# Two of four weight-block sums of a seven-product feed-forward stage, made by adding transfers from SBUF to SBUF instead of by VectorE

## The chip, the cores and the metric

The kernel runs on one core of a Trainium2 chip. The metric is the device time of one execution in microseconds; the kernel before has a median of 2433.65 us over three runs (2429.97 to 2434.26). Instructions and waits are read from one profiled execution, which took 2429.76 us.

## What is computed

One decoder layer over 512 positions of width 2048, in float32: a combined input projection, dilated attention and a pooling mixer, gates, an output projection, a normalisation, and a feed-forward part of hidden width 8192. The change is in the first matrix product of the last line but one:

```python
def reference(x, positions, w_in, w_pool, ..., w_ff1, w_ff2, ln_ff_g, ln_ff_b):
    ...
        x = layer_norm(DEEPNORM_ALPHA * x + mix, ln_mix_g[layer], ln_mix_b[layer])
        f = jnp.square(jax.nn.relu(x @ w_ff1[layer])) @ w_ff2[layer]
        x = layer_norm(DEEPNORM_ALPHA * x + f, ln_ff_g[layer], ln_ff_b[layer])
    return x
```

## The kernel before

Every matrix product works with float32 operands that are split into a high part, rounded to the matmul's format, and a low remainder: ScalarE writes the high part (line 87), VectorE subtracts it (line 88), and TensorE makes three products (high by high, high by low, low by high). For weights the parts are called wh and wl; both have three buffers, so the split of a piece can run at most two pieces ahead of the piece that TensorE works on.

The first feed-forward product runs by a scheme of seven products in place of eight (after Strassen and Winograd): the 512 positions are two halves, the 2048 rows of the weight two halves, and the hidden columns come in 16 groups of 512, each of two halves. Group 0 is made in the ordinary way; groups 1 to 15 are the units (class FUnit). A unit has four weight blocks, "11", "12", "21" and "22" (row half, column half), 128x2048 elements each, in four buffers (w1). It makes the products in the order M1, M5, M6, M3, M7, M2, M4. Each product is two pieces (FPiece, half of the rows each), so a unit has 14 pieces, j = 0 to 13, of 24 matmuls each.

The weights that M5, M6, M7 and M4 need are sums, made in place: 11 += 12 beside the splits of M1's pieces, 11 += 22 beside those of M5 (then M6 uses 11), 12 += 22 for M7, and 11 += 21 for M4. Each sum is two halves, one VectorE instruction of 128x1024 each (line 618).

The order of everything beside the matmuls is written out by hand, piece by piece: `fill` gives the splits up to piece j + 2, then `beside(u, j, last)` gives what belongs to piece j, and then the matmuls of piece j follow. `u.give(n, half)` hands a buffer on: it issues, on SyncE's queue, the load of the next unit's block into the half that is no longer used (line 613, 0.5 MB a load). The buffer of 22 is given at j = 4 and 6, that of 12 at j = 6 and 7, that of 21 at j = 8 and 9 and that of 11 at j = 10 and 11.

The result of a unit, the hidden blocks, is kept in one tile hpR: `block` (line 672) writes into it at j = 10, 12 and 13. During the next unit its combinations (line 548) are made and stored to memory for the second feed-forward product (`h_parts_out`, from line 550): at j = 5 and again at j = 7 ScalarE writes the high parts into hpH, a tile with one buffer, VectorE subtracts, and POOL stores both, h_parts<-hpH and h_parts<-hpR, 896 KB each (line 555). POOL's queue also carries the loads and stores of the residual rows (`y_load`, `y_rows`: lines 518 to 536). An engine works through its own queue strictly in order, so an instruction that waits holds up all behind it. SyncE's loads go through DMA queue q1, POOL's transfers through q0; both use the same 16 DMA engines.

Of the kernel before, what the change touches and what calls it, by code (L numbers as in the profile page):

```python
# [13 lines left out]
OP = mybir.AluOpType  # L14
# [54 lines left out]
def decoder_layer(ctx: ExitStack, tc: tile.TileContext, x, xt, positions, w_in, w_pool, pool_scale,  # L69
                  w_branch_attn, w_branch_pool, w_out, ln_mix_g, ln_mix_b, w_ff1, w_ff2,  # L70
                  ln_ff_g, ln_ff_b, consts, vectors, out, h_parts, h_rest, y_norm, y_parts):
    nc = tc.nc
# [443 lines left out]
    def y_load(t, n):  # L516
        c = slice(n * 512, (n + 1) * 512)
        nc.gpsimd.dma_start(low["u"][:, 1], y_norm[t, :, c])
        nc.gpsimd.dma_start(low["g"][:, 0], bcast(ln_mix_g, c))
        nc.gpsimd.dma_start(low["g"][:, 1], bcast(ln_mix_b, c))  # L520

    def y_rows(t, n):
        c = slice(n * 512, (n + 1) * 512)
        v, g, b = low["u"][:, 1], low["g"][:, 0], low["g"][:, 1]
        stt = nc.vector.scalar_tensor_tensor
        stt(v, v, ALPHA, g, op0=OP.mult, op1=OP.mult)
        stt(v, b, ALPHA, v, op0=OP.mult, op1=OP.add)
        if t >= 2 and n % 2:
            nc.gpsimd.dma_start(g, y_parts[t - 2, :, c])
            return lambda: y_rest(t, c)  # L530
        nc.gpsimd.dma_start(y_parts[t, :, c], v)
# [133 lines left out]
    def beside(u, j, last):  # L665

        v = {m: p.rearrange("p (n t) -> p n t", n=2) for m, p in u.ps.items()}
        m1, m5, u2 = low["m"][:, 0], low["m"][:, 1], low["u"][:, 0]
        act = nc.scalar.activation

        def block(slot, in0, in1, op):
            nc.vector.tensor_tensor(R[u.g][:, :, slot], in0.rearrange("p (n t) -> p n t", n=2), in1, op=op)

        def relu(a, b):
            act(R[u.g][:, :, a:b], R[u.g][:, :, a:b], AF.Relu)

        if j == 0:
            last.done()
        elif j == 2:
            act(m1, u.ps["M1"], AF.Copy)  # L680
        elif j == 4:
            act(m5, u.ps["M5"], AF.Copy, scale=-1.0)
            u.sum("12", "22", 0)
            u.give(0, 0)
        elif j == 6:
            act(u2, u.ps["M1"], AF.Copy, scale=-1.0)
            u.sum("12", "22", 1)
            u.give(0, 1)
            u.give(1, 0)
        elif j == 7:  # L690
            u.give(1, 1)
            if chunks:
                y_load(*chunks[0])
        elif j == 8:
            u.sum("11", "21", 0)
            u.give(2, 0)
        elif j == 9:
            u.sum("11", "21", 1)
            u.give(2, 1)
        elif j == 10:  # L700
            block(0, m5, v["M1"], OP.subtract)
            u.give(3, 0)
        elif j == 11:
            u.give(3, 1)
            if chunks:
                u.rest = y_rows(*chunks.pop(0))
        elif j == 12:
            block(1, u2, v["M5"], OP.subtract)
        elif j == 13:
            block(3, m1, v["M2"], OP.add)  # L710
            relu(0, 2)
        if j == 3 and last.rest:
            last.rest()
        if j in last.out:
            last.out[j]()
# [98 lines left out]
    def bcast(v, c=slice(0, DM)):  # L814
        return bass.AP(tensor=v.tensor, offset=v.offset + c.start, ap=[[0, P], [1, c.stop - c.start]])
# [188 lines left out]
    for p in fpieces:  # L1004
        fill(pos[2])
        beside(p.u, p.j, last)
        if p.u is funits[0] and p.j == 0:
            y_p3()
            funits[0].get("21")
        if p.u in funits[1:3] and p.j in (0, 4):  # L1010
            (y_load(*chunks[0]) if p.j == 0 else y_rows(*chunks.pop(0)))
        p.mult()
        pos[2] += 1
        if p.u is funits[-1] and p.j in (3, 5, 7):
            for m in {3: (0, 1), 5: (2, 3), 7: (4, 5)}[p.j]:
                h_load(0, m)
        if p.j == 13:
            last = p.u
# [89 lines left out]
```

## Time and profile before

| | value |
|---|---|
| median of three runs | 2433.65 us |
| the profiled execution | 2429.76 us |
| its span, first to last instruction | 2428.0 us |
| granted TensorE clock, mean | 0.997 |
| TensorE busy | 2392.9 us (99%) |
| VectorE busy | 1585.5 us (65%) |
| ScalarE busy | 963.1 us (40%) |
| POOL busy | 168.7 us (7%) |

The seven-product stage lies between about 1170 and 1793 us of the span. A unit takes some 41 us there, so a stretch of that length shows one turn of the order. TensorE's busy share counts waiting matmuls poorly, since matmuls overlap; the length of a unit and TensorE's listed waits tell more.

### The profile page before, as it was taken

What the parts mean: (1) busy time and instruction counts of PE and PEld (TensorE: products, weight loads), DVE (VectorE), ACT (ScalarE), POOL (GpSimd) and SP (SyncE); (2) the same over time, 40 slices, a digit from 0 to 9 for tenths busy, and PEclk for the clock granted to TensorE, in tenths of its full rate; (3) what the DMA queues carried; (4) which work ended last, traced back from release to release, by engine and by line L of the source; (5) the groups of instructions that cost most, each with busy time, mean ns of one, the idle gap of its engine ahead of it and who ended that gap; (6) DMA issues with size and microseconds to landing.
All of it is one profiled execution on the core that took longest, in us unless ns stands there. A gap on an engine that the chain in (4) does not pass through costs nothing.

```text
span 2428.0 us, 31729 instructions
## 1 busy us (share of the span) xinstructions
PE 2392.9 (99%) x13096; PEld 2078.2 (86%) x13096; DVE 1585.5 (65%) x1641; ACT 963.1 (40%) x1030; POOL 168.7 (7%) x256
## 2 busy tenths in 40 slices
PE   9999999999999999999899999999999999999998
PEld 7888888877788888888899999999988888888886
DVE  4532345555533334346888888888877988889886
ACT  4323311244432223126555555555554333333330
POOL 0000000000000000000112121111121000110000
PEclk9999999999999999999999999999999999999999
DMA  6232333222223333347577667676797556675642
GB/s 210 87 96 100 104 96 98 93 79 78 78 87 96 96 100 116 123 156 234 170 218 228 223 212 236 204 240 196 251 342 251 183 181 225 211 240 178 207 163 94
DMA packets 202880, 399.33 MB, mean 164 GB/s; under 512 B 12272, under 2 KB 74864, under 8 KB 201968
## 3 DMA queue, kind: packets, MB, share of 16 engines
q1 hardware_dynamic: 164272, 257.84, 33.0%
q0 software_dynamic: 36160, 135.28, 16.4%
q10 hardware_dynamic: 2304, 4.20, 0.5%
q8 instruction: 102, 1.67, 0.3%
q14 instruction: 42, 0.34, 0.0%
HBM read 329.11 MB, written 68.16 MB: 164 GB/s over the span
## 4 chain that ended last, share of the span: by engine, by line
PE 75%; issue 11%; DMA 6%; DVE 5%; ACT 2%; POOL 1%; POOLq 0%; SPq 0%; DVEq 0%; ACTq 0%
PE mm L147 43%; PE pp L800 20%; PE mm L663 5%; PE pp L845 4%; DMA w<-in_w_ff 2%; DVE wl L88 2%; DMA h_parts<-hpH 2%; DMA h_parts<-hpR 1%; DVE hpR L88 1%; PE sc L351 1%; PE tp L383 1%; ACT wh L87 1%; DMA low<-in_ln_mix_g 1%; ACT hpH L87 1%; DMA wr<-in_w_out 0%
## 5 line engine op out<-in xcount | busy, mean ns | idle before, releaser
L88 DVE TENSOR_TENSOR wl<-wr,wh 128x1024 fp32r<-128x1024 f32 (+1 forms) x228 | 277.5, 1220 | 566.9 <-ACT wh L87 566.3
L87 ACT ACTIVATE wh<-w 128x1024 fp32r<-128x1024 f32 x406 | 427.3, 1058 | 521.1 <-PE pp L800 295.0
L88 DVE TENSOR_TENSOR wl<-w,wh 128x1024 fp32r<-128x1024 f32 x406 | 494.5, 1221 | 109.6 <-ACT wh L87 107.8
L800 PE MATMUL pp<-wh,hop 128*128 128x512 f32 x1568 | 483.3, 389 | 1.2 <-ACT hpR L624 1.2
L87 ACT ACTIVATE wh<-wr 128x1024 fp32r<-128x1024 f32 (+1 forms) x228 | 240.4, 1055 | 611.4 <-PE mm L147 565.3
L147 PE MATMUL mm<-aH,wh 128*128 128x512 f32 (+1 forms) x1024 | 396.3, 387 | 1.3 <-ACT wh L87 1.3
L147 PE MATMUL mm<-aH,wl 128*128 128x512 f32 (+1 forms) x1024 | 386.8, 378 | 5.1 <-DVE wl L88 5.1
L147 PE MATMUL mm<-aL,wh 128*128 128x512 f32 (+1 forms) x1024 | 386.1, 377 | 0.0
L800 PEld LDWEIGHTS pp<-wh,hop 128*128 128x128 f32 x1568 | 294.4, 188 | 62.4 <-ACT hpR L624 1.4
L800 PE MATMUL pp<-wl,hop 128*128 128x512 f32 x784 | 305.4, 390 | 1.3 <-DVE wl L88 1.3
L663 PE MATMUL mm<-aH,wl 128*128 128x256 f32 x960 | 273.0, 284 | 7.0 <-DVE wl L88 7.0
L663 PE MATMUL mm<-aH,wh 128*128 128x256 f32 x960 | 271.9, 283 | 0.0
L663 PE MATMUL mm<-aL,wh 128*128 128x256 f32 x960 | 271.9, 283 | 0.0
L147 PEld LDWEIGHTS mm<-aH,wl 128*128 128x128 f32 x1024 | 193.5, 189 | 41.7 <-DVE wl L88 6.3
L147 PEld LDWEIGHTS mm<-aH,wh 128*128 128x128 f32 x1024 | 193.7, 189 | 39.1 <-ACT wh L87 2.5
L147 PEld LDWEIGHTS mm<-aL,wh 128*128 128x128 f32 x1024 | 193.8, 189 | 36.9 <-issue 1.9
L663 PE MATMUL mm<-ysH,wl 128*128 128x256 f32 x720 | 205.3, 285 | 6.0 <-DVE wl L88 6.0
L663 PE MATMUL mm<-ysH,wh 128*128 128x256 f32 x720 | 204.1, 283 | 0.0
L663 PE MATMUL mm<-ysL,wh 128*128 128x256 f32 x720 | 203.9, 283 | 0.0
L663 PEld LDWEIGHTS mm<-aH,wl 128*128 128x128 f32 x960 | 184.3, 192 | 8.7 <-DVE wl L88 8.4
L663 PEld LDWEIGHTS mm<-aH,wh 128*128 128x128 f32 x960 | 184.5, 192 | 0.0
L663 PEld LDWEIGHTS mm<-aL,wh 128*128 128x128 f32 x960 | 184.4, 192 | 0.0
(175 smaller groups left out, 3360.3 us busy)
## 6 DMA issues: line engine op xcount, KB each, us to landing
w<-in_w_ff SPq DMA_DIRECT2D x232, 512.0 KB, 10.8
wr<-in_w_in SPq DMA_DIRECT2D x127, 512.0 KB, 3.6
hop<-h_parts POOLq DMA_DIRECT2D x98, 512.0 KB, 7.1
h_parts<-hpH POOLq DMA_DIRECT2D x28, 896.0 KB, 9.3
h_parts<-hpR POOLq DMA_DIRECT2D x28, 896.0 KB, 9.2
wr<-in_w_out SPq DMA_DIRECT2D x40, 512.0 KB, 3.6
wr<-in_w_ff SPq DMA_DIRECT2D x32, 512.0 KB, 4.0
wr<-in_w_branch_pool SPq DMA_DIRECT2D x16, 512.0 KB, 3.7
```

Source lines behind the costliest of these rows:

```text
L87: nc.scalar.activation(dst_h, src, AF.Copy)
L88: nc.vector.tensor_tensor(dst_l, src, dst_h.bitcast(F32), op=OP.subtract)
L147: nc.tensor.matmul(o, l, r, start=first and j == 0, stop=last and j == 2)
L351: nc.tensor.matmul(p[:, :n], qT[h][:, qb * P:(qb + 1) * P], kT[h][:, :n], start=True, stop=True)
L383: nc.tensor.matmul(p[:, k * P:], vt["v"][:, k, h * HD:(h + 1) * HD], pT[h][:, k, k * P:], start=k == 0, stop=k == 3)
L663: nc.tensor.matmul(o, l, r, start=first, stop=self.j % 2 == 1 and k == 3 and i == 2, skip_group_check=True)
L800: nc.tensor.matmul(u.ps[:, t], l, r, start=q + j == 0, stop=q == 3 and j == 2)
L845: nc.tensor.matmul(o, l, r, start=first and i == 0, stop=last and i == 2)
```

## The change

In `beside`, the four instructions of a unit that add the second pair of sums are taken out, and two transfers take their place. They are issued by POOL and add their source to their destination, whole blocks at once (128x2048): 12 += 22 at j = 0 and 11 += 21 at j = 3. What is given on, and when, stays as it was.

```diff
         if j == 0:
             last.done()
+            nc.gpsimd.dma_start(u.b["12"], u.b["22"], accum_op=OP.add)
         elif j == 2:
             act(m1, u.ps["M1"], AF.Copy)
         elif j == 4:
             act(m5, u.ps["M5"], AF.Copy, scale=-1.0)
-            u.sum("12", "22", 0)
             u.give(0, 0)
         elif j == 6:
             act(u2, u.ps["M1"], AF.Copy, scale=-1.0)
-            u.sum("12", "22", 1)
             u.give(0, 1)
             u.give(1, 0)
         elif j == 7:
             u.give(1, 1)
             if chunks:
                 y_load(*chunks[0])
+        elif j == 3:
+            nc.gpsimd.dma_start(u.b["11"], u.b["21"], accum_op=OP.add)
         elif j == 8:
-            u.sum("11", "21", 0)
             u.give(2, 0)
         elif j == 9:
-            u.sum("11", "21", 1)
             u.give(2, 1)
```

VectorE's queue in the second unit, from the split of M3's first half on (w_ and a number name the four weight buffers), before:

```order
L88 TENSOR_TENSOR wl<-w_7708,wh 128x1024
L618 TENSOR_TENSOR w_7705<-w_7705,w_7708 128x1024
L88 TENSOR_TENSOR wl<-w_7708,wh 128x1024
L88 TENSOR_TENSOR hpR<-hpR,hpH 128x1792
L88 TENSOR_TENSOR wl<-w_7705,wh 128x1024
L618 TENSOR_TENSOR w_7705<-w_7705,w_7708 128x1024
L88 TENSOR_TENSOR wl<-w_7705,wh 128x1024
L88 TENSOR_TENSOR hpR<-hpR,hpH 128x1792
L88 TENSOR_TENSOR wl<-w_7869,wh 128x1024
L618 TENSOR_TENSOR w_7669<-w_7669,w_7869 128x1024
L88 TENSOR_TENSOR wl<-w_7869,wh 128x1024
L618 TENSOR_TENSOR w_7669<-w_7669,w_7869 128x1024
```

And the same stretch after:

```order
L88 TENSOR_TENSOR wl<-w_7708,wh 128x1024 x2
L88 TENSOR_TENSOR hpR<-hpR,hpH 128x1792
L88 TENSOR_TENSOR wl<-w_7705,wh 128x1024 x2
L88 TENSOR_TENSOR hpR<-hpR,hpH 128x1792
L88 TENSOR_TENSOR wl<-w_7870,wh 128x1024 x2
L88 TENSOR_TENSOR wl<-w_7669,wh 128x1024
```

The four L618 sums are gone and the splits and hpR subtractions keep their order.

POOL's queue over one later unit, before (in brackets the semaphores that a transfer waits for: DMAHW those of SyncE's loads, DMASW those of POOL's own transfers):

```order
L555 DMA h_parts<-hpH 128x7x256 [waits DMASW4_49,Activation_49]
L555 DMA h_parts<-hpR 128x7x256 [waits DMASW5_49,DVE_49]
L518 DMA low<-y_norm 128x512 [waits DMASW6_49,DMASW3_49]
L519 DMA low<-in_ln_mix_g 128x512 [waits DMASW7_49]
L520 DMA low<-in_ln_mix_b 128x512 [waits DMASW0_49]
L555 DMA h_parts<-hpH 128x7x256 [waits DMASW1_49,Activation_49]
L555 DMA h_parts<-hpR 128x7x256 [waits DMASW2_49,DVE_49]
```

And after:

```order
L679 DMA w_7705<-w_7708 128x2048 [waits DMAHW5_49,DMAHW6_49,DMAHW4_49,DMAHW7_49,DMASW2_49,DVE_49]
L694 DMA w_7669<-w_7870 128x2048 [waits DMAHW0_49,DMAHW1_49,DMASW3_49,DVE_49]
L555 DMA h_parts<-hpH 128x7x256 [waits DMASW4_49,Activation_49]
L555 DMA h_parts<-hpR 128x7x256 [waits DMASW5_49,DVE_49]
L518 DMA low<-y_norm 128x512 [waits DMASW6_49,DMASW1_49]
L519 DMA low<-in_ln_mix_g 128x512 [waits DMASW7_49]
L520 DMA low<-in_ln_mix_b 128x512 [waits DMASW0_49]
L555 DMA h_parts<-hpH 128x7x256 [waits Activation_49]
```

Both adding transfers (L679 and L694) stand ahead of the unit's four stores on POOL and wait for weight loads and for VectorE.

## Rows read from the trace of the kernel before

**Rows 1.** Windows: length, busy of PE, PEld, DVE, ACT, POOL; PEclk, DMA share, GB/s.
```profile
1215.77:1752.17 536.40, 528.40 (x4371) 525.18 (x4370) 462.36 (x437) 300.65 (x299) 85.80 (x115) 1.00 0.69 223
...
1384.70:1425.15 40.45, 40.45 (x339) 40.38 (x338) 35.10 (x34) 23.06 (x23) 6.13 (x8) 1.00 0.65 214
1589.71:1630.04 40.33, 40.33 (x338) 40.33 (x337) 36.08 (x35) 23.60 (x24) 6.13 (x8) 1.00 0.67 223
```

**Rows 2.** Waits of PE, 1215.77 to 1752.17: total us, times, longest us.
```profile
PE mm L663 <- DVE wl L88: 7.9, 11, 1.6
```

**Rows 3.** Groups by line: the sums (busy us, mean ns | idle before, releaser).
```profile
L618 DVE TENSOR_TENSOR w<-w,w 128x1024 f32<-128x1024 f32 x120 | 146.7, 1222 | 19.8 <-DMA w<-in_w_ff 18.0
```

**Rows 4.** Waits of ACT (1215.77 to 1752.17), then of SP (1190 to 1780).
```profile
ACT wh L87 <- DVE w L618: 90.8, 45, 4.9
...
SPq L613 <- DVE w L618: 423.4, 60, 19.0
```

**Rows 5.** Chain of waits, 1355 to 1390: start us, us, what.
```profile
1359.93 8.36 DMA h_parts<-hpH
...
1368.38 1.71 ACT hpH L87
...
1370.11 2.04 DVE hpR L88
```

**Rows 6.** Waits of PE, units of 1341.98 to 1384.70 and of 1425.15 to 1466.5.
```profile
PE mm L663 <- DVE wl L88: 1.9, 2, 1.6
...
PE mm L663 <- DVE wl L88: 0.6, 1, 0.6
```

**Rows 7.** DMA issues at 1402, 1359, 1442 and 1565: KB each, us to landing.
```profile
h_parts<-hpH POOLq DMA_DIRECT2D x1, 896.0 KB, 5.9
...
h_parts<-hpH POOLq DMA_DIRECT2D x1, 896.0 KB, 8.4
...
h_parts<-hpH POOLq DMA_DIRECT2D x1, 896.0 KB, 7.4
...
h_parts<-hpH POOLq DMA_DIRECT2D x1, 896.0 KB, 7.5
```

**Rows 8.** GB/s of all DMA, 1387 to 1404 in 40 equal slices.
```profile
GB/s 272 217 159 137 108 87 67 29 0 0 0 0 0 0 0 0 0 0 0 0 0 0 0 39 0 0 0 0 0 0 0 0 0 0 0 0 0 55 152 188
```

**Rows 9.** Timelines of DVE, SP, ACT, POOL about 1400: start us, us, engine, line.
```profile
1397.19 1.22 DVE L88 TENSOR_TENSOR wl<-w,wh 128x1024 fp32r<-128x1024 f32 x1
...
1401.95 0.37 SPq L613 DMA_DIRECT2D w<-in_w_ff  x1
...
1402.23 1.06 ACT L87 ACTIVATE wh<-w 128x1024 fp32r<-128x1024 f32 x1 [0.28 <-PE mm L663]
...
1402.25 0.97 POOL L555 DMA_DIRECT2D h_parts<-hpH  x1 [20.51 <-ACT hpH L87]
```

**Rows 10.** DMA queues, 1350 to 1473: packets, MB, share of 16 engines.
```profile
q0 software_dynamic: 4000, 14.68, 34.3%
q1 hardware_dynamic: 12672, 12.58, 32.3%
```

**Rows 11.** The same, 1404 to 1408.
```profile
q0 software_dynamic: 299, 1.16, 72.8%
```

**Rows 12.** Waits of DVE, then of ACT, 1215.77 to 1752.17.
```profile
DVE hpR L672 <- DMA h_parts<-hpR: 6.4, 6, 1.5
...
ACT hpH L87 <- DMA h_parts<-hpH: 5.5, 8, 1.7
```

**Rows 13.** Timeline of DVE, 1384.6 to 1394, in brackets the idle time before.
```profile
1384.57 0.69 DVE L672 TENSOR_TENSOR hpR<-low,mm 128x512 f32<-128x512 f32 x1 [1.30 <-DMA h_parts<-hpR]
...
1392.33 1.23 DVE L88 TENSOR_TENSOR wl<-w,wh 128x1024 fp32r<-128x1024 f32 x1 [1.68 <-ACT wh L87]
```

**Rows 14.** DMA queues and issues, 1407.7 to 1411.7.
```profile
q0 software_dynamic: 258, 0.97, 99.2%
...
w<-in_w_ff SPq DMA_DIRECT2D x2, 512.0 KB, 16.0
```

## The prediction

> **What bounds the kernel now.** I first read the windows of the first feed-forward stage. Over thirteen units of the seven-product scheme (1215.77 to 1752.17 us) TensorE is busy 528.4 of 536.4 us at a granted clock of 1.00 (the 2.4 GHz level), VectorE 462.4 us, and the 16 DMA engines 69% [rows 1]. One unit that nothing disturbs takes 40.33 us [rows 1], so thirteen would take 524.3 us: the stage has only 536.4 - 524.3 = 12.1 us, 0.93 us per unit, that any relief of VectorE could give back. The waits say that TensorE stands for one thing only, the low part wl that VectorE writes: 7.9 us in 11 waits [rows 2] (the rest of the 12.1 us is in smaller gaps). VectorE is 86% busy here, yet its own load is not what is late. I followed the chain of waits back from one such wait: POOL issues the store of the high parts of hidden blocks (h_parts<-hpH) at 1359.93; it lands 8.36 us later; only then may ScalarE write the next hpH into the same buffer (1.71 us), then VectorE subtracts (2.04 us) [rows 5], and the wl of the next piece stands behind that subtraction. In this unit TensorE waited up to 1.6 us, in the unit where the same store took 7.4 us it waited 0.6 us, and in the unit where it took 5.9 us it did not wait at all [rows 1, 6, 7]. So there is a limit of about 6.8 us from issue to landing (8.4 - 1.6 and 7.4 - 0.6), and each us above it is a us of TensorE. Call this **place A**. **Place B** is at the unit's end: VectorE's write of a hidden block into hpR (L672) waits for the last h_parts<-hpR store, 6.4 us in 6 waits [rows 12]; in one such case the write started at 1384.57 and the wl that ends the chain of VectorE and ScalarE work behind it started at 1392.33 [rows 13], and TensorE just did not have to wait for it (the unit of 1384.70 to 1425.15 is full [rows 1]). Both places hang on when stores land, not on how much VectorE adds.
>
> **What the change removes.** Four of the eight L618 sums of a unit leave VectorE: 60 of 120 in the stage, 1.222 us each [rows 3], so 60 x 1.222 = 73 us of VectorE, or 4.9 us per unit. ScalarE's waits for L618 (90.8 us) fall by perhaps half, and SyncE, which today waits for L618 before it may reload a buffer (423.4 us, 60 times) [rows 4], waits for VectorE's wl and for the adding transfer instead. All this lies between the sixth and the tenth piece. Place A's chain (landing, hpH, subtraction, wl) holds none of the removed sums, nor does place B's. So the gain that I count on TensorE's path is 0; the 12.1 us are its ceiling.
>
> **What it adds.** Two adding transfers per unit from POOL, 128x2048 f32 (1.05 MB) each; the trace of before has none, so I bound one from both sides. A plain pass of q0 cost 2.5 us per MB while stores ran (1.16 MB in 72.8% of 4 us) [rows 11], and 2.9 us per MB over three units (14.68 MB in 34.3% of 123 us) [rows 10]. The lower end is one pass, 1.05 x 2.5 = 2.6 us of all 16 engines; the upper is three passes (source, destination, write back, none overlapped) at 2.9, 9.1 us. I take two, since an add must read two tiles and a plain store already reads and writes in its one pass: 5.2 us. The Trainium skill ("Collectives: The Full Stack", Part 3) says the same of the reduce that DMA engines make: two source reads, the add itself free, at about 31 GB/s per engine; by it the estimate is 2 x 1.05 / (16 x 0.031) = 4.2 us, and the total below would be about 14 us less. No run here shows such an add yet.
>
> *First adding transfer (12 += 22).* It is issued once the buffers of 22 have landed. There the DMA engines fall idle: from about 1390 to 1402 hardly a byte moves [rows 8]. With 5.2 us of bytes and 3.6 us of overhead (a store's 5.9 us [rows 7] less 0.92 MB x 2.5) it lands some 9 us after issue, near 1399, ahead of the reload of 22 (1401.95) and of the first wh that reads 12 (1402.23) [rows 9]. That idle stretch is its cover; about 3 us are left, and past it each us delays M7 by one. Cost 0. On POOL, y_load stands behind it in the two units that load at their start; its rows are wanted four pieces later. Cost 0.
>
> *Second adding transfer (11 += 21).* It waits for the wl of M6's second half, which ends at 1397.19 + 1.22 = 1398.41; the hpH store follows on POOL at 1402.25 [rows 9], so its bytes stand 3.8 us behind in the same queue. The adding transfer needs 5.2 us, and the 0.5 MB reload issued at 1401.95 shares the engines (1.3 us): the store is pushed by 5.2 - 3.8 = 1.4 to 2.7 us; I take 2.0. **Place A:** landing 5.9 + 2.0 = 7.9, so 7.9 - 6.8 = 1.1 us of wait in a unit that does not wait today. Three of the thirteen units land it in 7.4 to 8.4 us today [rows 7]; there it is about 2.9 us. Mean (10 x 1.1 + 3 x 2.9) / 13 = 1.5 us. **Place B:** from the second adding transfer on, the engines have 5.2 us more to move and start 1401.95 - 1398.41 = 3.5 us earlier, so the last store lands 1.7 us later. Reloads freed about 3 us earlier by the missing sums compete with the stores: 0 if the stores keep the engines, as in the 4 us in which q0 had 99.2% while two loads had been issued [rows 14], or 1.5 us at an even share. I take 0.7, between the two, since over three units q1's packets take nearly as much time as q0's [rows 10]. The Trainium skill ("DMA: Bandwidth & Descriptors", Queues, rings and completion order) says that an engine goes round robin between its queues, packet by packet; by it the 1.5 us would hold, and the 4 us of the row above show otherwise. So the store lands 2.4 us later, of which TensorE has already stood 1.5 us at place A: 0.9 more.
>
> **Sum.** Per unit 1.5 (A) + 0.9 (B) + about 0.5 (the half of today's 0.93 that I put down to B, unchanged) = 2.9 us against 0.93 now: +2.0 us; over 14 units that store, +28 us. POOL's two more issues (under 1 us each, as its stores' are) and the other stages cost 0. The profiled execution took 2429.76 us (span 2428.0): 2429.8 + 28 = 2458. It lies 3.9 us below the median 2433.65, so the forecast on the median is **2462 us**.
>
> **Rivals.**
> *(1) The adding is slow.* Three passes, or an adder slower than the stream: q0 and q1 take 42.2 + 39.7 us of three units now [rows 10], 27.3 us per unit; with 2 x 9.1 that is 45.5 us and the DMA engines become the bound, +5.2 us per unit, +72 us: 2506; at 12 us per transfer 51.3 us, +150 us. For it: nothing in the trace prices an add. Against it: a stream that reads two tiles has no need of a third pass. It decides from about 6.5 us per transfer, where 27.3 + 2 x 6.5 reaches 40.3.
> *(2) Faster.* The adding costs about one pass (2.6 us) and is over before the store's bytes come; the reloads, free 3 us earlier, move in the stretch that is idle now, so the stores of the second half land earlier and both places close: up to 12 us less, 2422 to 2428. It decides where an adding transfer moves its bytes within the 3.8 us ahead of the store. For it: the idle stretch is there and VectorE gets 4.9 us per unit. Against it: it must do its two reads at twice the rate of q0's stores.
> *(3) No change.* Adding near 3.5 us: A is pushed by under 1 us, the earlier reloads give it back: 2429 to 2438.
>
> **How the numbers follow.** The forecast (slower, 2439 to 2506, likeliest 2462) gets 0.53, rival 1 beyond that 0.15, rival 2 0.18, rival 3 0.14. A measurement of this kernel can tell about 0.2% (4.9 us) from no change; so faster 0.18, same 0.14, slower 0.68. The range goes to 2424, which leaves out the better half of rival 2, and to 2520, which leaves out an adder at 10 us and more.
>
> **What would show it.** Right: VectorE's L618 group shows 60 sums, 73 us less; the undisturbed unit stays near 40.3 us but few are left; h_parts<-hpH from the unit's first half lands at 7.5 to 9 us, ScalarE's wait for it grows from 5.5 us to 20 us or more and VectorE's wait for h_parts<-hpR from 6.4 us [rows 12], TensorE's waits for wl reach 30 us or more, and the DMA share goes from 69% to about 90%. Wrong: an adding transfer that lands within 6 us of its issue and TensorE's waits at or below 7.9 us (rival 2 or 3); or adding transfers of 12 us and more, a stage near 100% DMA share, and M7's wh waiting for the first of them (rival 1).

## The result: 56 us slower, twice the forecast loss

The changed kernel takes 2490.0 us (median of four, 2488.0 to 2492.0), the kernel before 2433.86 us beside it: ratio 1.0236, 95% interval 1.0224 to 1.0248. The forecast was slower by 28 us (2462, range 2424 to 2520). The direction and the place held; the size was short by half.

**Where the time went.** The profiled execution took 2488.0 us, its span is 2486.2 us. Two windows of each trace split the span: the seven-product stage (units 1 to 15), and all that follows it. First the kernel before, then after; the columns are those of [rows 1].

```profile
1169.71:1790.26 620.55, 607.51 (x5018) 603.26 (x5017) 532.15 (x500) 349.58 (x351) 101.81 (x140) 1.00 0.69 222
1790.26:2428.00 637.74, 624.12 (x2762) 516.28 (x2760) 536.93 (x430) 234.97 (x222) 59.53 (x104) 0.99 0.59 203
```

```profile
1170.81:1840.36 669.55, 626.83 (x5017) 620.90 (x5017) 468.29 (x440) 350.57 (x351) 128.87 (x169) 0.97 0.85 250
1840.36:2486.20 645.84, 625.18 (x2762) 517.42 (x2760) 537.00 (x430) 235.27 (x222) 60.27 (x105) 0.99 0.59 203
```

The stage is 49.0 us longer, what follows 8.1 us, and what goes before 1.1 us. In the stage TensorE's idle time went from 620.55 - 607.51 = 13.0 us to 669.55 - 626.83 = 42.7 us: **29.7 us of waiting**. Its busy time rose by **19.3 us** for the same 5017 or 5018 matmuls, and the mean granted clock fell from 1.00 to 0.97. So the loss has three main parts: waits 29.7, busy time 19.3 (most of it slower matmuls, as shown below), the stage that follows 8.1.

**VectorE got what was meant, and TensorE nothing.** The sums in the lines of groups, and both transfers in the list of DMA issues of 1223.65 to 1761.08 (KB each, median us to landing):

```profile
L618 DVE TENSOR_TENSOR w<-w,w 128x1024 f32<-128x1024 f32 x60 | 73.5, 1225 | 2.1
```

```profile
w<-w POOLq DMA_DIRECT2D x24, 1024.0 KB, 8.3
h_parts<-hpH POOLq DMA_DIRECT2D x24, 896.0 KB, 9.4
h_parts<-hpR POOLq DMA_DIRECT2D x24, 896.0 KB, 10.3
```

60 sums are left of 120 [rows 3]: 73 us off VectorE. Its windows above show 63.9 us less in the stage.

**What TensorE waits for.** The waits of 1223.65 to 1761.08 (12 units), against [rows 2], [rows 4] and [rows 12], which cover thirteen units:

```profile
ACT hpH L87 <- DMA h_parts<-hpH: 70.3, 12, 7.3
...
PE mm L663 <- DVE wl L88: 20.1, 13, 1.8
...
PE mm L663 <- ACT wh L87: 12.9, 9, 2.3
...
DVE hpR L672 <- DMA h_parts<-hpR: 3.6, 3, 2.6
...
ACT wh L87 <- DVE w L618: 2.4, 2, 1.2
```

ScalarE's wait for the store h_parts<-hpH, 5.5 us before, is 70.3 us: once in each of the 12 units. TensorE waits 20.1 + 12.9 = 33.0 us, 2.75 us per unit, for the wl and the wh behind that. Place B's wait went down, from 6.4 to 3.6 us.

**One unit, step by step.** The chain of waits of 1455 to 1490, then the timelines of ScalarE, VectorE and TensorE:

```profile
1464.95 9.92 DMA h_parts<-hpH
...
1474.95 1.71 ACT hpH L87
...
1478.64 2.35 DVE wl L88 x2
```

```profile
1474.95 1.70 ACT L87 ACTIVATE hpH<-hpR 128x1792 fp32r<-128x1792 f32 x1 [6.55 <-DMA h_parts<-hpH]
1476.56 2.93 ACT L87 ACTIVATE wh<-w 128x1024 fp32r<-128x1024 f32 x3
...
1476.69 2.02 DVE L88 TENSOR_TENSOR hpR<-hpR,hpH 128x1792 f32<-128x1792 f32 x1 [7.03 <-ACT hpH L87]
...
1477.65 0.39 PE L663 MATMUL mm<-aH,wh 128*128 128x256 f32 x1 [1.59 <-ACT wh L87]
...
1479.90 0.58 PE L663 MATMUL mm<-aH,wl 128*128 128x256 f32 x1 [1.75 <-DVE wl L88]
```

It is the chain of [rows 5]. The store of the unit's first half lands 9.92 us after its issue; ScalarE, in order, stands 6.55 us before the next hpH, and the splits of the coming piece stand behind it: TensorE waits first for wh, then for wl.

**The prediction's limit of 6.8 us holds.** Over the 12 units the store of the first half lands 7.96, 8.01, 8.09, 9.30, 9.40, 9.64, 9.87, 9.92, 10.04, 10.07, 10.65 and 11.08 us after issue. Each less 6.8 us, summed, is 32.4 us; the waits measured are 33.0 us. The 0.6 us between the two are one wait, at 1544.96, that follows the longest wait of place B (2.6 us, to 1535.92).

**Behind the waits the clock falls.** Windows of a short unit, a long one, and three short stretches:

```profile
1405.29:1447.10 41.81, 40.58 (x339) 40.38 (x337) 30.70 (x30) 23.24 (x23) 7.98 (x10) 1.00 0.84 247
1447.10:1493.53 46.43, 43.09 (x338) 42.68 (x337) 31.76 (x31) 23.24 (x23) 8.52 (x11) 0.93 0.87 262
1478.24:1485.07 6.83, 5.17 (x24) 5.17 (x25) 4.48 (x5) 1.54 (x3) 1.01 (x1) 0.50 0.98 344
1420.00:1423.41 3.41, 3.41 (x30) 3.41 (x30) 2.18 (x2) 3.13 (x3) 0.69 (x1) 1.00 1.03 175
...
1570.40:1573.81 3.41, 3.41 (x18) 3.41 (x17) 2.12 (x3) 0.00 (x0) 0.00 (x0) 0.50 1.03 403
```

From the second of the two waits of the unit above on, the granted clock is 0.50, the level of 1.2 GHz, for 6.83 us. The last two rows are two stretches of equal length: 30 matmuls at full clock, 18 at that level. Ten stretches at 0.50, 44.4 us in all, lie in the stage; TensorE is busy for 39.6 us of them, with 192 matmuls. At the 40.33 us that 338 matmuls of an undisturbed unit take [rows 1], these would need 22.9 us. So some 16.7 of the 19.3 us are the clock's, by this estimate; where the other 2.6 us come from was not followed. Of the 12 units the three in which the store lands near 8 us, with one wait of 1.2 or 1.3 us, keep 1.00; the other nine, in which a wait for wh and one of some 1.75 us for wl stand close together, 2.2 us or more in all, show 0.93 or 0.96. Before, with waits of up to 1.6 us, no unit fell.

**The stage that follows.** Waits of 1836 to 1870:

```profile
PE pp L799 <- DVE wl L88: 8.4, 1, 8.4
DVE w L769 <- DMA w<-in_w_ff: 8.2, 1, 8.2
```

At the start of the second feed-forward product TensorE stands 8.4 us for a split, which stands behind a sum, which stands behind a weight load. That is about what this part of the span grew by (8.1 us).

### The profile page after: what moved, and what is told of

It is laid out like the page before. It is cut to its first block, busy times and chain, and to the rows that moved or that the text cites. A ratio compares the mean times of both kernels' runs of the same rounds, so it can differ in the third digit from the quotient of the medians.

```text
span 2486.2 us, 31779 instructions
## 1 busy us (share of the span) xinstructions
PE 2414.6 (97%) x13096; PEld 2098.0 (84%) x13096; DVE 1521.6 (61%) x1581; ACT 964.8 (39%) x1030; POOL 196.5 (8%) x286
## 4 chain that ended last, share of the span: by engine, by line
PE 74%; DMA 11%; issue 9%; DVE 3%; ACT 2%; POOL 1%; POOLq 0%; DVEq 0%; SPq 0%; ACTq 0%
PE mm L147 42%; PE pp L799 21%; DMA w<-in_w_ff 6%; DMA h_parts<-hpH 5%; PE mm L663 5%; PE pp L844 4%; DVE wl L88 2%; ACT hpH L87 1%; PE sc L351 1%; PE tp L383 1%; ACT wh L87 0%; POOL w L694 0%; PE tp L375 0%; DMA wr<-in_w_out 0%; PE tp L277 0%
## 5 line engine op out<-in xcount | busy, mean ns | idle before, releaser
L663 PE MATMUL mm<-aH,wl 128*128 128x256 f32 x960 | 281.8, 294 | 25.0 <-DVE wl L88 25.0
L663 PE MATMUL mm<-aH,wh 128*128 128x256 f32 x960 | 280.7, 292 | 14.9 <-ACT wh L87 14.9
L663 PE MATMUL mm<-aL,wh 128*128 128x256 f32 x960 | 279.2, 291 | 0.0
L147 PEld LDWEIGHTS mm<-aH,wl 128*128 128x128 f32 x1024 | 193.7, 189 | 41.5 <-DVE wl L88 6.2
L147 PEld LDWEIGHTS mm<-aH,wh 128*128 128x128 f32 x1024 | 193.9, 189 | 39.2 <-ACT wh L87 2.5
L147 PEld LDWEIGHTS mm<-aL,wh 128*128 128x128 f32 x1024 | 194.1, 190 | 37.1 <-issue 1.9
L663 PEld LDWEIGHTS mm<-aH,wl 128*128 128x128 f32 x960 | 192.3, 200 | 28.3 <-DVE wl L88 28.3
L663 PEld LDWEIGHTS mm<-aH,wh 128*128 128x128 f32 x960 | 192.4, 200 | 16.9 <-ACT wh L87 16.9
L663 PEld LDWEIGHTS mm<-aL,wh 128*128 128x128 f32 x960 | 192.1, 200 | 0.0
## 6 DMA issues: line engine op xcount, KB each, us to landing
h_parts<-hpR POOLq DMA_DIRECT2D x28, 896.0 KB, 10.3
```

Of the source, the lines that this page charges most:

```text
L147: nc.tensor.matmul(o, l, r, start=first and j == 0, stop=last and j == 2)
L663: nc.tensor.matmul(o, l, r, start=first, stop=self.j % 2 == 1 and k == 3 and i == 2, skip_group_check=True)
```

## The experiments

In all of them "before" is the kernel before, run beside them. The table gives each run's ratio with its interval and, from its profiled execution, the windows of the stage (length, TensorE's idle and busy time in it) and of what follows. A longer busy time is not the clock alone: e7's is 6.7 us above that of before at a mean clock of 1.00. The experiments come in the order of the questions they answer.

| kernel | us | ratio [95%] | stage | idle | busy | after the stage |
|---|---|---|---|---|---|---|
| before | 2433.9 | | 620.6 | 13.0 | 607.5 | 637.7 |
| changed kernel | 2490.0 | 1.0236 [1.0224, 1.0248] | 669.6 | 42.7 | 626.8 | 645.8 |
| e3 no third and fourth sum | 2428.7 | 0.9981 [0.9971, 0.9991] | 622.2 | 13.4 | 608.8 | 637.2 |
| e1 first transfer only | 2428.1 | 0.9984 [0.9974, 0.9993] | 619.0 | 13.0 | 606.0 | 637.4 |
| e2 second transfer only | 2475.4 | 1.0171 [1.0156, 1.0187] | 657.7 | 33.8 | 623.9 | 647.9 |
| e5 second reload later | 2475.4 | 1.0178 [1.0162, 1.0195] | 655.6 | 32.7 | 622.9 | 646.1 |
| e6 both reloads later | 2476.1 | 1.0182 [1.0164, 1.0199] | 658.4 | 35.4 | 623.0 | 646.5 |
| e7 as e1, both reloads later | 2440.0 | 1.0035 [1.0021, 1.0048] | 632.8 | 18.6 | 614.2 | 636.9 |
| e4 second transfer behind the stores | 2474.2 | 1.0169 [1.0153, 1.0184] | 667.6 | 45.9 | 621.8 | 636.7 |
| e8 half of the second transfer | 2431.5 | 1.0003 [0.9991, 1.0015] | 619.7 | 11.8 | 607.9 | 641.8 |
| e12 three quarters of it | 2461.7 | 1.0119 [1.0098, 1.0139] | 646.6 | 27.9 | 618.7 | 644.8 |
| e10 second transfer in two halves | 2449.0 | 1.0066 [1.0047, 1.0084] | 632.3 | 21.1 | 611.2 | 644.3 |
| e9 last unit's second sum by VectorE | 2479.7 | 1.0195 [1.0178, 1.0212] | 675.4 | 44.7 | 630.7 | 636.7 |
| e11 e8, last unit by VectorE | 2428.9 | 0.9985 [0.9975, 0.9996] | 620.1 | 12.2 | 607.8 | 637.6 |

The theory at the start: the second adding transfer, with the reloads set free earlier, pushes the store of place A. The rivals: the adding bytes as such fill the DMA engines, or the first transfer holds back M7.

**What is VectorE's relief worth (e3), and what does each transfer cost (e1, e2)?** e3 leaves out the third and the fourth sum and adds nothing in their place, so it does not compute the layer.

```diff
-            nc.gpsimd.dma_start(u.b["12"], u.b["22"], accum_op=OP.add)
...
-        elif j == 3:
-            nc.gpsimd.dma_start(u.b["11"], u.b["21"], accum_op=OP.add)
```

> The third and the fourth sum are left out altogether (M7 takes 12 and M4 takes 11 without them): VectorE's relief and the earlier reloads alone, with no adding transfer. Theory: the adding's bytes are the cause, so 2420 to 2436 us, with TensorE's waits in the stage at or below today's 8 us in thirteen units. Rival (the earlier reloads, two of which go ahead of the store of hpH, are cause enough): 2445 us or more, the store landing at 8 us or later.

2428.68 us: 0.19% less than before, with 73 us of VectorE gone and no byte added. The ceiling of the whole idea is some 4 us.

e1 keeps the first transfer and gives the second sum back to VectorE; e2 does the reverse.

```diff
-        elif j == 3:
-            nc.gpsimd.dma_start(u.b["11"], u.b["21"], accum_op=OP.add)
         elif j == 8:
+            u.sum("11", "21", 0)
             u.give(2, 0)
         elif j == 9:
+            u.sum("11", "21", 1)
             u.give(2, 1)
```

> Only the first adding transfer (12 += 22); VectorE makes 11 += 21 as before. Theory (place A: the second adding transfer, with the reloads, stands ahead of the store of hpH): the first one runs in the idle stretch, so the median stays near that of before, 2424 to 2440 us, and the store h_parts<-hpH of a unit's first half lands in under 7.5 us after its issue. Rival (what counts is the DMA work added, wherever it stands): half of the loss, 2455 to 2465 us.

```diff
         if j == 0:
             last.done()
-            nc.gpsimd.dma_start(u.b["12"], u.b["22"], accum_op=OP.add)
...
+            u.sum("12", "22", 0)
             u.give(0, 0)
         elif j == 6:
...
+            u.sum("12", "22", 1)
             u.give(0, 1)
```

> Only the second adding transfer (11 += 21); VectorE makes 12 += 22 as before, so the second half's reload of 22 is freed as late as before. Theory: the larger part of the loss, 2455 to 2485 us; without the early second reload the store of hpH is pushed less than after the change (landing near 8 us, not 9.5 to 11). Rival (DMA work): half of the loss, 2455 to 2465, with landings as after the change.

The first transfer is free: e1 takes 2428.13 us, a gain of 0.16%, though some of its stores land later than the 7.5 us expected, at up to 8.5 us. The DMA engines are busy for 80% of its stage, against 69% before, and it loses nothing by it. The second alone costs 43 us. The first costs 14.6 us only where the second is there too (2490.0 against 2475.4); e5 asks why.

**Why does the first transfer cost something beside the second (e5, e6, e7)?** In the unit of 1405.29 to 1447.10 of the changed kernel SyncE issues its first two reloads here, 14.0 and 16.8 us into the unit:

```profile
1419.31 0.37 SPq L613 DMA_DIRECT2D w<-in_w_ff  x1
...
1422.12 0.37 SPq L613 DMA_DIRECT2D w<-in_w_ff  x1
```

POOL's adding transfer and store of the same unit:

```profile
1417.24 0.86 POOL L694 DMA_DIRECT2D w<-w  x1 [9.87 <-DVE wl L88]
1422.72 1.01 POOL L555 DMA_DIRECT2D h_parts<-hpH  x1 [4.62 <-ACT hpH L87]
```

In the kernel before, in the unit that starts at 1384.70, the first goes out at 1401.95 [rows 9] and the second here, 17.3 and 22.6 us in:

```profile
1407.29 2.90 SPq L613 DMA_DIRECT2D w<-in_w_ff  x3
```

Before, SyncE stood for the sums (423.4 us, [rows 4]); with no sum to wait for, both reloads now go out ahead of the store; before, the store (1402.25, [rows 9]) went out ahead of the second. e5 lets the second reload stand behind a later one in SyncE's queue.

```diff
-            u.give(0, 1)
             u.give(1, 0)
+            u.give(0, 1)
```

> The changed kernel with one order on SyncE's queue altered: the reload of 22's second half goes behind that of 12's first half, so it is issued at about 20 us into a unit instead of 16.8, behind the store of hpH (17.4). Theory (two reloads of 1.3 to 1.5 us each go ahead of the store, on top of the second adding transfer): the store lands some 1.5 us earlier, about 1 to 1.5 us less wait per unit and fewer falls of the clock, 2460 to 2477 us. Rival (the adding transfer alone pushes the store): 2485 to 2493 us.

2475.42 us: 14.6 us less than the changed kernel, and as much as e2 takes, in which VectorE still makes 12 += 22 and SyncE's second reload goes out some 23 us into the unit, as before. So the 14.6 us that the first transfer costs here are the second reload's early issue. e6 moves the first reload too, and e7 does that to e1.

```diff
-            u.give(0, 0)
         elif j == 6:
...
-            u.give(0, 1)
             u.give(1, 0)
+            u.give(0, 0)
+            u.give(0, 1)
```

> The changed kernel with both reloads of 22 behind that of 12's first half. The store of hpH then follows directly on the second adding transfer, whose bytes end near 18.9 us into a unit. Theory: landing 6 to 7 us after issue in most units, place A nearly closed, 2432 to 2450 us. Rival (the adding transfer alone): place A stays, 2475 us or more.

> Only the first adding transfer, as in the run that had it alone (2428 us), with both reloads of 22 behind that of 12's first half. Theory (reloads ahead of the store are what keeps place A alive there: landings of 5.9 to 8.5 us, 7.9 us of TensorE's waits): landings near 5 to 6 us, 2418 to 2425 us, if the later loads are not missed at the unit's end. Rival (place B takes over): 2426 to 2432 us.

Both missed. The stores came sooner (in e6 those of the first half land in 6.3 to 7.9 us), but a new wait took over. Waits of e6, 1223 to 1750, and of e7:

```profile
ACT wh L87 <- DMA w<-in_w_ff: 77.9, 18, 8.3
...
PE mm L663 <- DVE wl L88: 20.5, 27, 1.6
```

```profile
ACT wh L87 <- DMA w<-in_w_ff: 68.2, 20, 5.8
...
PE mm L663 <- DVE wl L88: 12.8, 21, 0.8
```

The reloads now land too late for the next unit's first splits. They have slack, but not of a whole issue slot.

**Is it the bytes, or where they stand (e4, e8, e12, e10)?** e4 issues the second transfer behind the stores of the first half (j = 5).

```diff
-        elif j == 3:
-            nc.gpsimd.dma_start(u.b["11"], u.b["21"], accum_op=OP.add)
...
         if j in last.out:
             last.out[j]()
+        if j == 5:
+            nc.gpsimd.dma_start(u.b["11"], u.b["21"], accum_op=OP.add)
```

> Both adding transfers, the second issued on POOL behind the two stores of the unit's first half instead of ahead of them. Theory (what stands ahead of the store): the store of hpH lands in about 6 to 8 us again (the early reload still goes ahead), place A costs 1 us a unit or less, 2435 to 2460 us. Rival (DMA work): no change, 2480 to 2495 us, with place B (VectorE waiting for h_parts<-hpR) in place of A.

2474.2 us; the theory's 2435 to 2460 missed. Waits of e4, 1223 to 1750:

```profile
ACT wh L87 <- DMA w<-w: 61.6, 12, 6.5
...
ACT hpH L87 <- DMA h_parts<-hpH: 43.2, 12, 4.8
DVE hpR L672 <- DMA h_parts<-hpR: 29.1, 12, 4.9
PE mm L663 <- DVE wl L88: 19.6, 22, 2.9
```

Place A eased (hpH of the first half lands in 6.1 to 8.6 us). The push went on to the stores of the second half (hpH lands in 12.6 to 15.3 us, against 10.2 to 12.9 before), so place B appeared, and M4 now waits for its own sum (61.6 us). Moved, not removed.

e8 leaves the transfer at j = 3 but gives it half the rows; VectorE adds the others. e12 gives it three quarters.

```diff
-            nc.gpsimd.dma_start(u.b["11"], u.b["21"], accum_op=OP.add)
+            nc.gpsimd.dma_start(u.b["11"][:, :4], u.b["21"][:, :4], accum_op=OP.add)
...
         elif j == 9:
+            u.sum("11", "21", 1)
```

> Both adding transfers, the second for the first half of the rows only (half the bytes, about 2.6 us of all engines); VectorE adds the other half. By the forecast's point of decision (bytes within the 3.8 us ahead of the store) the loss nearly goes: 2430 to 2445 us. Rival (any transfer there costs, in proportion): half of the loss, 2455 to 2465 us.

```diff
-            nc.gpsimd.dma_start(u.b["11"][:, :4], u.b["21"][:, :4], accum_op=OP.add)
+            nc.gpsimd.dma_start(u.b["11"][:, :6], u.b["21"][:, :6], accum_op=OP.add)
...
-            u.sum("11", "21", 1)
+            nc.vector.tensor_tensor(u.b["11"][:, 6:], u.b["11"][:, 6:], u.b["21"][:, 6:], op=OP.add)
```

> The second adding transfer carries three quarters of its rows (0.79 MB, by the share of the whole transfer's 5.2 us some 3.9 us of all engines), VectorE adds the last quarter. The store's bytes stand 3.8 us behind. Theory (each us by which the store lands beyond about 6.8 us costs TensorE a us, and half-speed stretches come only with long waits): the store lands at 7 to 8.5 us, 0.5 to 1.5 us of wait per unit, no half-speed stretch; with 4 us or more behind the stage 2440 to 2458. Rival (it is the number of transfers or of passes that counts, not how long they run): as with the half, 2428 to 2434, or as with the whole, 2470 and more.

Issues of e8 and of e12, 1223 to 1750 (KB each, median us to landing):

```profile
w<-w POOLq DMA_DIRECT2D x12, 1024.0 KB, 7.3
w<-w POOLq DMA_DIRECT2D x13, 512.0 KB, 4.5
```

```profile
w<-w POOLq DMA_DIRECT2D x12, 1024.0 KB, 7.1
w<-w POOLq DMA_DIRECT2D x13, 768.0 KB, 7.0
```

With half (512 KB) the stage loses nothing, 619.7 us; with three quarters 26 us, with the whole 49. Half the transfer lands 4.5 us after its issue, and the store is issued 6.0 to 7.7 us after the transfer; three quarters land after 7.0 us, and the store is issued 3.5 to 5.9 us after it. Each quarter beyond the half costs the stage some 25 us. e12 came out somewhat above the theory's 2440 to 2458: the store landed in 6.7 to 10.6 us, later than the 7 to 8.5 expected, and the busy time grew by 11.2 us at a mean clock of 0.98, where the theory had expected no fall of the clock. Both rivals of e12 are out too.

e10 keeps all the bytes, but in two halves, the second behind the stores of the first half.

```diff
-            nc.gpsimd.dma_start(u.b["11"], u.b["21"], accum_op=OP.add)
+            nc.gpsimd.dma_start(u.b["11"][:, :4], u.b["21"][:, :4], accum_op=OP.add)
...
+        if j == 5:
+            nc.gpsimd.dma_start(u.b["11"][:, 4:], u.b["21"][:, 4:], accum_op=OP.add)
```

> The second adding transfer is cut in two: the half for the first rows stays at j = 3, the half for the last rows is issued at j = 5 behind the stores of the first half. Bytes per unit are those of the changed kernel. Theory (what counts is how much stands ahead of a store): place A is as in the run with half a transfer, the stores of the second half are pushed by half of what the run with the whole transfer behind the stores showed, so 2435 to 2460. Rival (the bytes of two adding transfers are too much for the stage wherever they stand): 2470 to 2490, as with the whole transfer at either place.

2449.0 us, as the theory had it: the stage of e10 at a higher DMA share loses 11.8 us where the changed kernel loses 49.

```profile
1171.48:1803.79 632.31, 611.18 (x5018) 605.22 (x5017) 465.32 (x438) 348.24 (x351) 143.51 (x185) 1.00 0.89 266
```

0.89 against 0.85: it isn't the bytes of a unit that bound the stage, but how many of them stand ahead of a store that ScalarE waits for.

**What are the 8 us behind the stage (e9, e11)?** The last unit's second sum goes back to VectorE, in the changed kernel (e9) and in e8 (e11).

```diff
-        elif j == 3:
+        elif j == 3 and u.g < 15:
             nc.gpsimd.dma_start(u.b["11"], u.b["21"], accum_op=OP.add)
         elif j == 8:
+            if u.g == 15:
+                u.sum("11", "21", 0)
             u.give(2, 0)
         elif j == 9:
+            if u.g == 15:
+                u.sum("11", "21", 1)
             u.give(2, 1)
```

> The changed kernel, but in the last seven-product unit VectorE makes 11 += 21 again. Theory: the 8.4 us for which TensorE waits at the start of the second product, and the 6.8 us at half clock behind it, belong to the last unit's second adding transfer alone; both go, so about 8.4 plus half of 6.8, some 8 to 12 us less than the changed kernel (2478 to 2482), and the stage of the other units is as before. Rival: the wait belongs to the reloads of that stage whatever makes the sum, and the time stays at 2488 to 2492.

> The run with half of the second sum by transfer, but in the last unit VectorE makes all of 11 += 21. With the half, the seven-product stage took 619.7 us against 620.6 before and what follows it 641.8 against 637.7. Theory: those 4 us belong to the last unit's half transfer; they go, and the kernel takes 2425 to 2429, as much under the kernel before as the version with the first adding transfer alone. Rival: the stage's profile was a lucky one, and the time stays at 2429 to 2433.

e9 takes 2479.7 us, 10.3 us less. What follows its stage is back at 636.7 us (637.7 before, 645.8 with the change), and TensorE's wait of 8.4 us is gone. (Its profiled execution took 2484.3 us, the longest of its four, hence the longer stage in the table.) e11 takes 2428.9 us, and behind its stage 637.6 us against e8's 641.8. So these 8 us belong to the last unit's second transfer alone. POOL's timeline of the changed kernel shows where it stands, and the chain of waits of 1800 to 1880 what is late:

```profile
1817.67 1.24 POOL L694 DMA_DIRECT2D w<-w  x1
```

```profile
1837.44 23.29 DMA w<-in_w_ff
...
1860.86 0.09 DVE w L769
```

In that unit the transfer is issued 14.7 us after the unit's start (1802.92), among the loads of the second product. The weight load for which the sum waits at 1860 is not issued late: it goes out 2.9 us before the stage ends, as the last of these eight loads does in the kernel before and in e9. But it lands 23.3 us after its issue, against 16.0 us before and 14.0 us in e9. So the time is lost between issue and landing; which of the other transfers hold this load up was not followed further.

Two whole versions are below the kernel before by 0.15%, at the edge of what a measurement can tell: e1 (2428.1) and e11 (2428.9). Both reach what e3 gets without any of these sums (2428.7), so more than that isn't there. e1 is the simpler.

## Why the prediction was right or wrong, step by step

**What bounds the kernel: right.** VectorE's relief is worth 3.4 us (e3), under the ceiling of 12.1 us from [rows 1]. Place A is where the waits arise, and its limit of 6.8 us gives them to within a us (32.4 against 33.0 us).

**The price of an adding transfer: right.** Taken as two passes, 5.2 us of all engines. The DMA queues of 1406 to 1414 of the changed kernel, where the first transfer runs nearly alone:

```profile
q0 software_dynamic: 145, 1.05, 64.7%
```

64.7% of 8 us is 5.2 us for 1.05 MB. The Trainium skill ("Collectives: The Full Stack", Part 3) explains the two passes by two source reads; the trace agrees with the two, and at 1.05 MB in 5.2 us of 16 engines it is 12.6 GB/s of result per engine, somewhat less than half of that section's 31. Rival 1 is out: it asked for over 6.5 us.

**First transfer 0: right.** e1 shows it, and e2 with e5 that its price beside the second is a reload's.

**Second transfer, the push at place A: the term that was mis-sized.** The prediction pushed the store by 2.0 us, of which 1.3 us for one reload. Taking the undisturbed 5.9 us of [rows 7], it was pushed by 2.1 to 5.2 us, most often by near 4: median (9.64 + 9.87) / 2 = 9.75 us to landing. The queues of 1419 to 1424.2, of 1425.6 to 1427.3 and of 1427.3 to 1431 in the unit of 1405.29, one of the mild ones (8.0 us), show the order:

```profile
q0 software_dynamic: 112, 0.92, 107.7%
...
q1 hardware_dynamic: 627, 0.63, 106.6%
...
q0 software_dynamic: 331, 1.29, 87.8%
q1 hardware_dynamic: 228, 0.22, 17.1%
```

First the adding transfer alone (L694, issued 1417.24), though two loads were issued at 1419.31 and 1422.12; then the loads alone, though the store was issued at 1422.72; only then the store. The store stood 5.5 us behind the adding transfer here, not 3.8, and landed 8.0 us after issue; where it stood 3.5 us behind (1550.07 and 1553.60), it landed 11.1 us after issue. Two reloads stood ahead of it, not one. The prediction knew that the missing sums free them about 3 us earlier, but put that down to place B alone; it did not read out of SyncE's order that the second would pass the store too. e5 prices this at 14.6 us of the 56. An even share between the queues, the upper end that the prediction kept, is not what these rows show: for microseconds on end one queue has the engines whole. The Trainium skill ("DMA: Bandwidth & Descriptors", Queues, rings and completion order) has an engine change between its queues packet by packet, and a packet there is typically 9 to 17 descriptors. The prediction took that for an even share. But the adding transfer's 112 pieces in the first row are 0.92 MB, so all its 1.05 MB are some 128 pieces, 8 for each of 16 engines: by that rule an engine may well finish its whole part before it turns to the loads, and these rows don't speak against it.

Place A so cost 32.4 / 12 = 2.7 us per unit, not 1.5.

**Place B: wrong.** Forecast to grow by 0.9 us per unit; its wait fell from 6.4 to 3.6 us. The prediction had a unit's last store, h_parts<-hpR of the second half, land later. From its issue it landed sooner: in 9.2 to 12.8 us, median 9.9, against 11.0 to 13.5, median 12.3, before. In e5, in which only the second reload goes out later, it takes 10.6 to 14.4 us, median 12.4, and VectorE waits for it again (1223 to 1750):

```profile
DVE hpR L672 <- DMA h_parts<-hpR: 18.0, 8, 4.2
```

So the early reload that is dear at place A clears place B, which the prediction allowed for in rival 2 alone. The two errors cancel: forecast 2.9 us of waits per unit, measured 33.0 / 12 = 2.75. For the stage the forecast was 28 us of waiting, the measured growth 29.7 us. That this term came out right is luck.

**Not priced at all: the clock, some 17 us.** The prediction had no term for it. In the stage before, waits of up to 1.6 us left the granted clock at 1.00; with the change, two longer waits close together did not. This is three tenths of the loss. What decides whether the clock falls stays open: in e4 TensorE idles 45.9 us, more than in the changed kernel, with its waits in other places of the unit, and the mean clock of its stage is 0.99.

**"The other stages cost 0": wrong by 8.1 us**, in the last unit, whose second transfer meets the second product's loads (e9, e11). The prediction counted 14 units that store and left out the fifteenth.

The measured parts, 29.7 + 19.3 + 8.1 and 1.1 us ahead of the stage, are the 58.2 us by which the profiled span grew. Of these the prediction had the first, and that came out right by two errors. So the step that left the forecast at half the loss is what it put at nothing: the lower clock behind the waits, some 17 us, and the last unit's second transfer, 8.1 us.

**The point of decision: right in kind, not in size.** Rival 2 was to win where the adding transfer moves its bytes within 3.8 us ahead of the store. Half the bytes (2.6 us) costs nothing (e8); three quarters, 3.9 us by the same rate and so just past the limit, already costs 29.5 us (e12). So the turn lies between 2.6 and 3.9 us; where, no run shows.

Of the signs named: VectorE's L618 group as said; landings at 7.5 to 9 us forecast, 8.0 to 11.1 measured; ScalarE's wait 20 us or more, 70.3; TensorE's waits for wl 30 us or more, 20.1 and 12.9 for wh; DMA share about 90%, 85%. VectorE's wait for h_parts<-hpR was to grow and did not.

## What to carry to other kernels

A transfer that takes work from an engine with slack gains what that engine's slack was worth; measure that first by leaving the work out (here 4 us). What it costs is set by what it stands ahead of in the queues: ask how many us of bytes there are before the next store that someone waits for, and put no more than that there; cut in two it may fit. When a wait goes, list every transfer that the wait held back, and where each now stands. And waits of TensorE can cost more than their length: here 29.7 us more of waiting came with some 17 us more at the lower clock, in e4 32.9 us more of it with a mean clock that hardly fell (0.99).

## What the runs showed of the hardware

- An adding transfer of 1.05 MB within SBUF takes 5.2 us of all 16 engines, twice a store's 2.5 us per MB [rows 11], and lands 6.9 to 11.7 us after issue.
- While it ran, 0.92 MB in 5.2 us, loads that had been issued on the other queue for up to 4.9 us moved no packet; then 0.63 MB of theirs went in 1.7 us while a store stood issued. In that stretch the queues had the engines one after the other, in the order of issue.
- With two waits of 1.59 and 1.75 us close together, TensorE was granted 0.50 for 6.83 us from the second on; with a single wait of 1.2 us in the unit before it, 1.00 throughout.
